# A hybrid decoder block on one core: weight forms kept between the token halves, down thirds alternating, and first-half products on x before its norm

## The chip, the cores and the metric

The kernel runs on one core of one Trainium2 chip. The metric is device time in microseconds (us) of one execution. TensorE is PE in the profile, VectorE is DVE, ScalarE is ACT, GpSimd is POOL, SyncE is SP; SP issues nearly all DMAs.

## The reference

One block over 2048 tokens of width 1024, all in fp32. What matters here:

```
u    = rms_norm(x, norm1_gain)
proj = u @ w_in                      # 1024 -> 3072: lru, gate, q, k, v, g
y_lru = rms_norm(rg_lru(conv4(x_lru)) * gelu(g_lru))
q, k = rotary(q), rotary(k)
y_ret = head_norm(retention(q, k, v)) * silu(g_ret)
h    = x + [y_lru, y_ret] @ w_out
u    = rms_norm(h, norm2_gain)
up   = conv3(u @ ffn_up_w)           # 1024 -> 6144
h    = h + (gelu(a) * v) @ ffn_down_w   # 3072 -> 1024
out  = rms_norm(h, final_norm_gain)
```

The norm of x is a number per token times a gain per channel. A projection is linear, so the number per token may be applied to x or to the projection's output.

## The kernel before

Activations are kept channel-major: a tile has 128 channels on the partitions and 1024 tokens, one half of the sequence (g = 0 or 1). A fp32 product is made of three matmuls on parts: a value is split into a rounded high part (a copy on ACT into the type float32r) and a low part (a subtraction on DVE), and high x high, high x low and low x high are summed in PSUM.

The matrix products are cut into units. A unit multiplies a pair of weight tiles (two groups of 128 output channels, 1024 input channels) with the 1024 tokens of a half. A plain unit (PlainUnit, line 712) does it in eight products of 12 matmuls of 512 columns. A sum-form unit (Unit, line 589) does it in seven, on sums and differences of blocks in the manner of Strassen: its activations are the blocks 11, 21, 22 and the differences T1 to T4 (Blocks, Blocks.put); its weights are one tile as it is (a), two tiles of half sums (s1, s2) and a half tile (v), each split into high and low part (weights, sums). Three low parts and three casts of 1024 columns and four half sums of 512 columns make the forms of one unit, besides v. A unit leaves PSUM through u2, c11, c22, c21 and c12 of PlainOut: ACT copies, and two DVE sums.

The stages follow one another: A (g = 0, four plain units on x times gain, whose outputs are multiplied by the norm's number per token, rb1, while they leave PSUM), AS (g = 0, eight sum-form units, on blocks of the normed x), AS (g = 1, twelve sum-form units), B (output projection, four plain units for each half), U (up projection, 24 sum-form units for each half), D (down projection in three thirds c of the hidden width, four units for each; the three thirds of g = 0, then the three of g = 1). The last unit is plain, in smaller pieces. ORDER names the units of A and AS: l is a channel group of the recurrent branch, q a head's q and k, v a head's v and gate. Every third's partial sum is stored in DRAM and loaded again as the residual of the next (AddOut, partial).

The sum-form blocks of x come from make_x (line 1050): for each pair of tiles it loads x, waits for rb1, multiplies by gain and rb1 on DVE, forms T1 to T4, and stores the seven blocks in DRAM; a stage's bring loads a block, casts and subtracts it.

Nothing of the order is written by hand. A planner (Flow) runs while the program is built: each step is a process with a priority, a tick of 12 matmuls that it is due at, and the planner gives each engine's next instruction by a table of costs and by priority, to 55 slots of 4 KB per partition in SBUF and 8 PSUM banks. The engines then run their instructions in that order, each waiting on semaphores for what it needs. An instruction that PE reaches before its input is there stops PE, since PE takes its matmuls in order.

The lines that matter for the clock of the work:

```
PRODUCTS = ((-4, "p1", "11"), (-2, "p5", "T1"), (0, "p6", "T2"), (1, "p2", "21"), (2, "p7", "T3"),
            (4, "p4", "T4"), (6, "p3", "22"))
```

At the end of a recurrent group (LruGroup.add, line 1163) the sum of squares over four channel groups goes through 16 matmuls of one column (rstd, tile mst), issued on PE among the products.

Of the kernel before, what the change touches and what calls it, by code (L numbers as in the profile page):

```python
# [15 lines left out]

# [1 line left out]

# [14 lines left out]
KT = D // P  # L33
# [19 lines left out]
CH = 4  # L53
ISSUE = 0.45
CL = 100
NDUE = 3
LESS = 0
XSTEP = 6
# [269 lines left out]
def hymba_block_kernel(ctx: ExitStack, tc: tile.TileContext, xh, xn, win, wout, wup, down, gates, vecs,  # L328
# [59 lines left out]
    class Blocks:  # L388
# [2 lines left out]

        names = ("11", "T1", "T2", "21", "T3", "T4", "22")

        def __init__(self, name, more=()):
            self.names = self.names + more
# [155 lines left out]
    class RawStage(Stage):  # L551
# [6 lines left out]
        def bring(self, name, i, need, start):  # L558
# [27 lines left out]
                free(r)  # L586
            self.event(name, i).on = True

    class Unit:


# [4 lines left out]
        def __init__(self, stage, wsrc, out):  # L596
            self.stage, self.wsrc, self.out = stage, wsrc, out
            self.w = {}
            self.there = {n: Event() for n in ("a", "s1", "s2", "v")}
            self.done = {n: Event() for n in ("seed", "u2", "c11", "c22a", "c22b")}  # L600
            out.unit = self

        def weights(self, t0):
            self.t0 = t0
# [83 lines left out]

        def p2(self):
            yield from self.product(self.x, "a", "12", "21", False)  # L690
            free(*self.w["a"])
            fl.spawn(self.out.c11(), self.t0 + 1.9 - SOON)

        def p7(self):
            yield self.done["u2"]
            yield from self.product(self.y, "s1", "3", "T3", False)
            free(*self.w["s1"])
            fl.spawn(self.out.c22(), self.t0 + 2.5 - SOON)

        def p4(self):  # L700
            yield self.done["c22a"]
            yield from self.product(self.y, "v", "v", "T4", False)
            free(self.w["v"])
            fl.spawn(self.out.c21(), self.t0 + 6 - LESS)

        def p3(self):
            yield self.done["c22b"]
            yield from self.product(self.e, "s2", "4", "22", False)
            free(*self.w["s2"])
            fl.spawn(self.out.c12(), self.t0 + 8 - LESS)  # L710

    class PlainUnit:


        period = 8
        quads = ((0, 0), (0, 1), (1, 0), (1, 1))
# [4 lines left out]
        def __init__(self, stage, wsrc, out):  # L721
            self.stage, self.wsrc, self.out = stage, wsrc, out
            self.w = {}
            self.there = [[Event(), Event()] for m in range(2)]
            self.placed = [Event(), Event()]
            out.unit = self
            out.quads = {}

# [48 lines left out]
        def part(self, q, m, n, k, c0=None, c1=None):  # L777
            if c0 is None:
                c0, c1 = n * Q, (n + 1) * Q
            if k == 0:  # L780
                PlainUnit.count += 1
                self.ps = yield Bank(self.tags[PlainUnit.count % 5], "pq")
            yield self.there[m][k]
            bname = f"{k + 1}{n + 1}"
            wh, wl = self.w[m]
            op = None
            for j in range(4):
                if j % 2 == 0:
                    yield self.stage.event(bname, j // 2)
                bh, bl = self.stage.blk[bname, j // 2]  # L790
                c = slice(j % 2 * Q + c0 - n * Q, j % 2 * Q + c1 - n * Q)
                ws = slice((4 * k + j) * P, (4 * k + j + 1) * P)
                for i, (x, y) in enumerate(((wh, bh), (wh, bl), (wl, bh))):
                    mm = pe.matmul(self.ps[:, 0:c1 - c0], x[:, ws], y[:, c], start=k == 0 and j == 0 and i == 0,
                                   stop=k == 1 and j == 3 and i == 2)
                    op = op + mm if op else mm
                if self.halves:
                    yield op
                    op = None
            if op:  # L800
                yield op
            self.stage.used(bname)
            if k == 1:
                if m not in [x[0] for x in self.quads[q + 1:]]:
                    free(*self.w[m])
                fl.spawn(self.leave(m, n, c0, c1), self.t0 + 2 * q + 4 - SOON)

        def leave(self, m, n, c0, c1):
# [28 lines left out]
    class PlainOut:  # L837


        def quadrant(self, m, n, ps):  # L840
# [17 lines left out]
            if (m, 0) in q and (m, 1) in q:  # L858
# [3 lines left out]
                else:  # L862
                    self.t1 = q[m]
                    yield from self.first()

        def u2(self):
# [22 lines left out]
        def c21(self):  # L889
            u = self.unit  # L890
            yield a.copy(self.t2[:, half(0)], u.y)
            free(u.y)
            yield u.done["c22b"]
            yield from self.second()

        def c12(self):
            u = self.unit
            t = self.t1[:, half(1)]
            yield v.tensor_tensor(out=t, in0=t, in1=u.e, op=ALU.add)
            free(u.e)  # L900
            yield u.done["c11"]
            yield from self.first()

    class AddOut:
# [135 lines left out]

    rb1 = {}
    rb_there = [Event() for g in range(NG)]
    rb_left = [KT + 4 * PLAIN] + [KT] * (NG - 1)

    def rb_used(g):
        rb_left[g] -= 1
# [138 lines left out]
    class Head:  # L1185


        def __init__(self, g, h):
            self.g, self.h = g, h
            self.t = {}  # L1190
            self.rope = None
            self.rope_there = Event()
# [2 lines left out]
        def rotate(self, name, x):  # L1195
            sw = yield Slot("sw")
            yield dma(sw[0:64], x[64:128]) + dma(sw[64:128], x[0:64])
            if self.rope is None:
                self.rope = []
                for i in range(2):  # L1200
                    t = yield Slot("rope")
                    self.rope.append(t)
                    yield dma(t, rope[self.g, i])
                self.rope_there.on = True
            yield self.rope_there
            cs, sn = self.rope
# [139 lines left out]
            free(s)  # L1346

    class QkOut(PlainOut):
        def __init__(self, head):
            self.head, self.g = head, head.g  # L1350

# [122 lines left out]
    class UpOut(PlainOut):  # L1474
# [22 lines left out]
        def first(self):  # L1497
# [7 lines left out]
            if self.j % 2 == 0:  # L1505
                even[0] = ca
            else:
                yield t0 + 14
                yield from g_d[self.g][self.j // 8].put(self.j // 2 % 4, even[0], ca)

    even = [None]


    def stage_a(g):
        plain = RawStage("A", g, x_d[g], V_N1)
        st = Stage("AS", g, x_b[g])
        us = []
        group = LruGroup(g)

        def add(i, j, out):  # L1520
            kind, stage = (PlainUnit, plain) if g == 0 and len(us) < PLAIN else (Unit, st)
            us.append(kind(stage, (win[i], win[j]), out))

        heads = [Head(g, h) for h in range(NH)]
        for what in ORDER[g].split():
# [22 lines left out]

    def stage_u(g):
        st = Stage("U", g, u_d[g])  # L1550
        return st, [Unit(st, (wup[j], wup[NF + j]), UpOut(g, j)) for j in range(NF)]

    def stage_d(g, c):
        st = Stage("D", g, g_d[g][c])
# [12 lines left out]
            free(t)  # L1567

        us = []
        for m in range(KT // 2):  # L1570
            ms = (m, m + KT // 2)
            src = [(h_d[g][c][k // 2], k % 2) for k in ms]
            done = (lambda i, t, ms=ms: ng.add(ms[i], t)) if c == 2 else (lambda i, t, ms=ms: partial(ms[i], t))
            out = AddOut(src, done)
            out.pieces = lambda i, t, c0, c1, ms=ms: ng.piece(ms[i], t, c0, c1)
            kind = LastUnit if final and m == KT // 2 - 1 else Unit
# [11 lines left out]
    with tc.manual_schedule():  # L1588
# [2 lines left out]
        fl.spawn(constants(), 3)  # L1591
        table = {}
        end = 0
        last = None
        for i, (st, us) in enumerate(order):
            if last is PlainUnit and type(us[0]) is Unit:
                end += 4
            if st.kind == "A":
                norm1(0, -200, end + NDUE)
                make_x(0, 0, end + XD0)  # L1600
            elif st.kind == "AS" and st.g:
# [96 lines left out]
```

## Time and profile before

| | us |
|---|---|
| median of 3 runs (2181.4 to 2182.86) | 2182.34 |
| the profiled execution | 2183.93 |
| its span, first to last instruction | 2182.1 |
| PE busy | 2152.2 |
| PE weight loads busy | 1773.1 |
| DVE busy | 1764.3 |
| ACT busy | 1245.9 |

The profile is of one execution. A matmul's busy time includes the filling and emptying of the array, so that consecutive matmuls overlap in it. Every instruction is put down to line 127 or 365, the helpers that record them, so that groups are told apart by the names of their tiles: px, py, pe and pq are PSUM tiles of products; wh and wl (wv) high and low parts of weights; bh and raw, bl those of blocks; s a tile of half sums; o an output.

### The profile page before, as it was taken

How to read it: one execution, taken by the hardware profiler on the slowest of the kernel's cores; microseconds unless marked ns; L12 is line 12 of the kernel's file. 1: busy time of each engine (PE TensorE's matmuls, PEld its weight loads, DVE VectorE, ACT ScalarE, POOL GpSimd, SP SyncE). 2: the span in 40 equal slices, each digit the busy share in tenths (PEclk: the TensorE clock that was granted, in tenths of full speed). 3: DMA queues.
4: the chain of work that ended last, by engine and by line, in shares of the span. 5: the costliest groups of instructions: out<-in, count | busy, mean ns of one | idle time of the engine just before them, and what ended most of it. 6: DMA issues, size and time to landing. Idle time of an engine off the chain costs nothing.

```text
span 2182.1 us, 26589 instructions
## 1 busy us (share of the span) xinstructions
PE 2152.2 (99%) x9848; PEld 1773.1 (81%) x9848; DVE 1764.3 (81%) x2227; ACT 1245.9 (57%) x1792; POOL 39.3 (2%) x32
## 2 busy tenths in 40 slices
PE   9999989999999999999999999999999999999998
PEld 6878878888788888888888888888888788888787
DVE  6999888877765688898888898788878987788875
ACT  6774775654852166666666766666666553343441
POOL 0010000000000000000000000000000000000000
PEclk9999999999999999999999999999999999999999
DMA  8966365142647954453224532322335787689662
GB/s 323 373 228 207 109 222 167 61 137 70 224 164 263 374 191 167 166 177 130 100 91 155 193 121 97 116 90 97 112 118 177 264 314 254 227 295 398 230 255 78
DMA packets 142498, 411.00 MB, mean 188 GB/s; under 512 B 16112, under 2 KB 20640, under 8 KB 142368
## 3 DMA queue, kind: packets, MB, share of 16 engines
q1 hardware_dynamic: 141072, 408.25, 52.8%
q8 instruction: 77, 1.26, 0.2%
q10 hardware_dynamic: 1296, 1.05, 0.1%
q14 instruction: 53, 0.43, 0.1%
HBM read 275.78 MB, written 125.07 MB: 184 GB/s over the span
## 4 chain that ended last, share of the span: by engine, by line
PE 94%; DVE 3%; DMA 2%; ACT 1%; POOL 0%; issue 0%; SPq 0%; DVEq 0%
PE py L127 33%; PE px L127 22%; PE pe L127 22%; PE pq L127 12%; PE po L127 1%; DMA raw<-in_dram 1%; PE pa L127 1%; PE pt L127 1%; PE pk L127 1%; PE sc L127 1%; DVE raw L127 1%; PE mst L127 1%; DMA xt<-in_dram 0%; DVE res L127 0%; DMA h<-h 0%
## 5 line engine op out<-in xcount | busy, mean ns | idle before, releaser
L127 DVE TENSOR_TENSOR wl<-s,wh 128x1024 fp32r<-128x1024 f32 x182 | 222.2, 1221 | 108.8 <-ACT wh L127 106.5
L127 PE MATMUL px<-bh,wh 128*128 128x512 f32 x728 | 287.2, 395 | 0.4 <-DVE res L127 0.4
L127 PE MATMUL py<-bh,wl 128*128 128x512 f32 x728 | 284.0, 390 | 2.8 <-DVE wl L127 2.8
L127 PE MATMUL px<-raw,wh 128*128 128x512 f32 x728 | 285.0, 391 | 0.3 <-DVE raw L127 0.3
L127 PE MATMUL py<-bh,wh 128*128 128x512 f32 x728 | 285.2, 392 | 0.0
L127 PE MATMUL pe<-raw,wh 128*128 128x512 f32 x728 | 283.4, 389 | 1.6 <-DVE raw L127 1.6
L127 PE MATMUL pe<-bh,wh 128*128 128x512 f32 x728 | 284.8, 391 | 0.0
L127 PE MATMUL px<-bh,wl 128*128 128x512 f32 x728 | 284.7, 391 | 0.0
L127 PE MATMUL py<-raw,wh 128*128 128x512 f32 x728 | 283.8, 390 | 0.3 <-DVE raw L127 0.3
L127 PE MATMUL pe<-bh,wl 128*128 128x512 f32 x728 | 283.5, 389 | 0.0
L127 ACT CAST wh<-s 128x1024 fp32r<-128x1024 f32 x182 | 190.9, 1049 | 140.8 <-DVE s L127 127.2
L127 DVE SCALAR_TENSOR_TENSOR c<-o,vec,c 128x1022 f32<-128x1022 f32 x192 | 244.1, 1279 | 9.0 <-ACT c L127 4.6
L127 PE MATMUL py<-bh,wv 128*128 128x512 f32 x728 | 240.4, 391 | 3.4 <-ACT o L127 1.7
L127 ACT COPY o<-py 128x512 f32<-128x512 f32 x204 | 119.6, 587 | 198.1 <-PE py L127 197.7
L127 DVE TENSOR_TENSOR raw<-raw,bh 128x1024 fp32r<-128x1024 f32 x158 | 189.2, 1217 | 7.0 <-ACT bh L127 7.0
L127 ACT CAST bh<-raw 128x1024 fp32r<-128x1024 f32 x158 | 161.5, 1048 | 35.7 <-DMA raw<-g_T 14.4
L127 PE MATMUL pq<-bh,wh 128*128 128x512 f32 (+1 forms) x432 | 168.0, 389 | 0.5 <-ACT bh L127 0.4
L127 PEld LDWEIGHTS px<-bh,wh 128*128 128x128 f32 x728 | 137.8, 189 | 35.3 <-issue 3.8
L127 PE MATMUL pq<-bh,wl 128*128 128x512 f32 (+1 forms) x432 | 165.0, 382 | 0.5 <-DVE wl L127 0.5
L127 PEld LDWEIGHTS py<-bh,wv 128*128 128x128 f32 x728 | 136.7, 188 | 34.1 <-ACT o L127 2.2
L127 PEld LDWEIGHTS py<-bh,wl 128*128 128x128 f32 x728 | 136.8, 188 | 31.8 <-DVE wl L127 3.2
L127 PEld LDWEIGHTS px<-bh,wl 128*128 128x128 f32 x728 | 137.5, 189 | 29.0
(143 smaller groups left out, 3819.1 us busy)
## 6 DMA issues: line engine op xcount, KB each, us to landing
wa<-in_dram SPq DMA_DIRECT2D x91, 512.0 KB, 4.6
wb<-in_dram SPq DMA_DIRECT2D x91, 512.0 KB, 5.2
h<-res SPq DMA_DIRECT2D x56, 512.0 KB, 3.4
g_T<-t SPq DMA_DIRECT2D x96, 256.0 KB, 2.5
raw<-g_T SPq DMA_DIRECT2D x48, 512.0 KB, 7.0
res<-h SPq DMA_DIRECT2D x48, 512.0 KB, 7.7
g<-c SPq DMA_DIRECT2D x76, 256.0 KB, 3.4
raw<-g SPq DMA_DIRECT2D x38, 512.0 KB, 7.9
```

Of the source, the lines that this page charges most:

```text
L127: return Op(self.name, lambda: fn(*args, **kw), us, writes, reads, func=func)
```

## The change

Three things change.

1. *Weight forms kept.* If two units that follow one another have the same weight tiles and the same kind, the second takes over the forms of the first (same), which doesn't free them (keep). For this the orders are turned so that the second half starts with the weights that the first half ended with: ORDER, B in reverse for g = 1, U for g = 1 starting with its last two units, D starting with its last. The thirds of D alternate: c = 0 for g = 0, 1; c = 1 for g = 1, 0; c = 2 for g = 0, 1. The pairing of the up projection's outputs (twin) follows.
2. *First-half sum-form units on x without its norm.* For g = 0, make_x multiplies by the gain alone, on ACT, and stores T1 to T4 only; the blocks 11, 21 and 22 are those of the plain units (MixedStage, kind AM), which stay in SBUF. The outputs of the AM units are multiplied by rb1 on DVE after they have left PSUM (times_rb).
3. *Rotary tables normed.* For the q/k units of AM that multiplication is left out and the two rotary tables are multiplied by rb1 once, stored in DRAM and loaded by those heads (scaled_rope).

In ORDER, l3 also moves to the end of the first half.

```diff
-ORDER = ("l0 q0 v0 l1 q1 v1 l2 q2 v2 l3 q3 v3", "l0 q0 v0 l1 q1 v1 q2 v2 l2 q3 v3 l3")
+ORDER = ("l0 q0 v0 l1 q1 v1 l2 q2 v2 q3 v3 l3", "l3 q0 v0 l0 q1 v1 q2 v2 l1 q3 v3 l2")
...
+ROPE_T = 16
...
-    x_b = [Blocks(f"x{g}") for g in range(NG)]
+    x_b = [Blocks(f"x{g}", names=("T1", "T2", "T3", "T4") if g == 0 else None) for g in range(NG)]
+    rope_d = Dram("rope")
...
+    class MixedStage(Stage):
+        def __init__(self, plain, g, src):
+            super().__init__("AM", g, src)
+            self.plain = plain
+            self.blk = ChainMap(self.blk, plain.blk)
+        def event(self, name, i):
+            return (super() if name[0] == "T" else self.plain).event(name, i)
...
+        def same(self, other):
+            self.w, self.there, self.weights = other.w, other.there, self.begin
+            other.keep = True
...
+        def drop(self, *tiles):
+            if not self.keep:
+                free(*tiles)
...
+        def times_rb(self, t):
+            if self.unit.stage.kind == "AM" and not self.scaled:
+                yield rb_there[self.g]
+                yield v.tensor_tensor(out=t, in0=t, in1=rb1[self.g], op=ALU.mult)
+                rb_used(self.g)
...
             yield u.done["c22b"]
+            yield from self.times_rb(self.t2)
             yield from self.second()
...
             yield u.done["c11"]
+            yield from self.times_rb(self.t1)
             yield from self.first()
...
+    def scaled_rope():
+        yield Until(ROPE_T)
+        yield rb_there[0]
+        for i in range(2):
+            t = yield Slot("rope")
+            yield dma(t, rope[0, i])
+            yield v.tensor_tensor(out=t, in0=t, in1=rb1[0], op=ALU.mult)
+            rb_used(0)
+            yield from rope_d.put(i, t)
+            free(t)
...
-            yield rb_there[g]
-            for j in range(2):
-                yield v.scalar_tensor_tensor(out=t[j], in0=t[j], scalar=col(V_N1 + 2 * q + j), in1=rb1[g], op0=ALU.mult, op1=ALU.mult)
-                rb_used(g)
+            if g == 0:
+                for j in range(2):
+                    yield a.activation(t[j], t[j], AF.Copy, scale=gain1[:, 2 * q + j:2 * q + j + 1])
+            else:
...
-                    yield dma(t, rope[self.g, i])
+                    if self.scaled:
+                        yield from rope_d.get(t, i)
+                    else:
+                        yield dma(t, rope[self.g, i])
...
-        st = Stage("AS", g, x_b[g])
+        st = Stage("AS", g, x_b[g]) if g else MixedStage(plain, g, x_b[g])
...
-        for m in range(KT // 2):
+        for m in (range(KT // 2) if g == 0 else reversed(range(KT // 2))):
...
-        return st, [Unit(st, (wup[j], wup[NF + j]), UpOut(g, j)) for j in range(NF)]
+        js = list(range(NF)) if g == 0 else [NF - 1, NF - 2, *range(NF - 2)]
+        return st, [Unit(st, (wup[j], wup[NF + j]), UpOut(g, j)) for j in js]
...
-        for m in range(KT // 2):
+        for m in (range(KT // 2) if g == c % 2 else (KT // 2 - 1, *range(KT // 2 - 1))):
...
-    order += [stage_d(g, c) for g in range(NG) for c in range(3)]
+    order += [stage_d(g, c) for c in range(3) for g in (range(NG) if c != 1 else reversed(range(NG)))]
...
+                if before and type(before) is last and [w.offset for w in before.wsrc] == [w.offset for w in u.wsrc] and \
+                        before.wsrc[0].tensor.name == u.wsrc[0].tensor.name:
+                    u.same(before)
+                before = u
```

## Rows read from the trace of the kernel before

**Rows 1.** The page: busy share of each engine; one group of matmuls.

```profile
PE 2152.2 (99%) x9848; PEld 1773.1 (81%) x9848; DVE 1764.3 (81%) x2227; ACT 1245.9 (57%) x1792; POOL 39.3 (2%) x32
...
L127 PE MATMUL px<-raw,wh 128*128 128x512 f32 x728 | 285.0, 391 | 0.3 <-DVE raw L127 0.3
```

**Rows 2.** Windows: length, busy us (instructions) by engine, PEclk, DMA share, GB/s.

```profile
240.00:280.00 40.00, 40.00 (x218) 34.45 (x217) 38.41 (x67) 23.12 (x30) 2.39 (x2) 1.00 0.40 133
...
880.00:1280.00 400.00, 400.00 (x1767) 331.20 (x1766) 346.52 (x386) 266.07 (x433) 0.00 (x0) 1.00 0.42 144
...
2120.00:2140.00 20.00, 19.24 (x85) 15.59 (x84) 9.44 (x11) 4.58 (x5) 0.00 (x0) 1.00 0.16 53
```

**Rows 3.** Chain of work that ended last: start us, us, what.

```profile
125.01 4.54 PE px L127 x12
147.65 3.48 PE py L127 x10
...
316.69 3.54 PE mst L127 x16
320.24 4.26 PE px L127 x12
...
1707.42 2.73 PE px L127 x12
```

**Rows 4.** PE's waits over the span: us in total, times, longest us.

```profile
PE mst L127 <- DVE sqacc L127: 7.5, 2, 6.3
PE py L127 <- DVE wl L127: 2.8, 1, 2.8
...
PE py L127 <- ACT o L127: 1.7, 1, 1.7
PE py L127 <- DVE res L127: 1.7, 2, 0.9
PE pe L127 <- DVE raw L127: 1.6, 1, 1.6
...
PE pa L127 <- DVE xc L127: 0.9, 1, 0.9
```

**Rows 5.** Narrow windows after two of the waits, columns as in rows 2.

```profile
125.00:130.00 5.00, 5.00 (x15) 3.56 (x16) 5.00 (x7) 2.62 (x5) 0.00 (x0) 0.66 0.60 216
...
320.00:325.00 5.00, 5.00 (x18) 3.97 (x18) 4.72 (x7) 0.46 (x1) 2.01 (x1) 0.69 0.00 0
```

**Rows 6.** DVE by form, 0 to 330 us: count, busy, mean ns, idle before.

```profile
L127 DVE TENSOR_TENSOR raw<-raw,bh 128x1024 fp32r<-128x1024 f32 x26 | 31.1, 1215 | 1.8 <-ACT bh L127 1.7
L127 DVE TENSOR_TENSOR wl<-s,wh 128x1024 fp32r<-128x1024 f32 x19 | 23.1, 1215 | 1.0 <-ACT wh L127 1.0
L127 DVE SCALAR_TENSOR_TENSOR x<-x,vec,rb 128x1024 f32<-128x1024 f32 x16 | 19.9, 1277 | 0.0
...
L127 DVE TENSOR_TENSOR s<-s,wa 128x512 f32<-128x512 f32 x10 | 6.9, 686 | 0.1
```

**Rows 7.** ACT by form, 0 to 330 us, columns as in rows 6.

```profile
L127 ACT CAST bh<-raw 128x1024 fp32r<-128x1024 f32 x28 | 28.5, 1047 | 1.8 <-PE po L127 1.8
...
L127 ACT ACTIVATE ea<-tt,m8sp 128x1024 f32<-128x1024 f32 x4 | 4.6, 1155 | 0.1
```

**Rows 8.** Wide windows, columns as in rows 2.

```profile
40.00:150.00 110.00, 106.16 (x489) 84.06 (x488) 103.15 (x143) 77.36 (x99) 6.26 (x3) 0.98 0.79 287
160.00:320.00 160.00, 153.66 (x761) 126.87 (x759) 137.54 (x204) 103.47 (x137) 4.78 (x4) 0.98 0.58 191
1940.00:2020.00 80.00, 79.31 (x358) 65.14 (x356) 63.77 (x77) 27.60 (x33) 1.64 (x1) 1.00 0.93 353
```

**Rows 9.** DMA issues, 0 to 330 us: count, KB each, median us to landing.

```profile
raw<-x SPq DMA_DIRECT2D x12, 512.0 KB, 7.5
```

**Rows 10.** The page's DMA issues over the span, columns as in rows 9.

```profile
h<-res SPq DMA_DIRECT2D x56, 512.0 KB, 3.4
...
res<-h SPq DMA_DIRECT2D x48, 512.0 KB, 7.7
```

More of the change, by code (lines that the diff above doesn't have):

```diff
@@ L19 @@
+from collections import ChainMap
 from contextlib import ExitStack
@@ L392, in hymba_block_kernel, with __init__ @@
         names = ("11", "T1", "T2", "21", "T3", "T4", "22")
-        def __init__(self, name, more=()):
-            self.names = self.names + more
+        def __init__(self, name, more=(), names=None):
+            self.names = (names or self.names) + more
             self.t = {(n, i): dp.tile([P, 2, Q], F32, name=f"{name}_{n}_{i}", tag=f"{name}_{n}_{i}")
@@ L587, in bring, with uses, used @@
             self.event(name, i).on = True
+    class MixedStage(Stage):
[5 more added lines that the diff above has]
+            return (super() if name[0] == "T" else self.plain).event(name, i)
+        def uses(self, name, tick):
+            (super() if name[0] == "T" else self.plain).uses(name, tick)
+        def used(self, name):
+            (super() if name[0] == "T" else self.plain).used(name)
     class Unit:
@@ L600, in __init__, with begin @@
             self.done = {n: Event() for n in ("seed", "u2", "c11", "c22a", "c22b")}
+            self.keep = False
             out.unit = self
+        def same(self, other):
+            self.w, self.there, self.weights = other.w, other.there, self.begin
+            other.keep = True
+        def begin(self, t0):
+            self.t0 = t0
+        def drop(self, *tiles):
+            if not self.keep:
+                free(*tiles)
         def weights(self, t0):
@@ L690, in p2 @@
             yield from self.product(self.x, "a", "12", "21", False)
-            free(*self.w["a"])
+            self.drop(*self.w["a"])
             fl.spawn(self.out.c11(), self.t0 + 1.9 - SOON)
@@ L696, in p7 @@
             yield from self.product(self.y, "s1", "3", "T3", False)
-            free(*self.w["s1"])
+            self.drop(*self.w["s1"])
             fl.spawn(self.out.c22(), self.t0 + 2.5 - SOON)
@@ L702, in p4 @@
             yield from self.product(self.y, "v", "v", "T4", False)
-            free(self.w["v"])
+            self.drop(self.w["v"])
             fl.spawn(self.out.c21(), self.t0 + 6 - LESS)
@@ L708, in p3 @@
             yield from self.product(self.e, "s2", "4", "22", False)
-            free(*self.w["s2"])
+            self.drop(*self.w["s2"])
             fl.spawn(self.out.c12(), self.t0 + 8 - LESS)
     class PlainUnit:
+        same, begin, drop = Unit.same, Unit.begin, Unit.drop
         period = 8
@@ L725, in __init__ @@
             self.placed = [Event(), Event()]
+            self.keep = False
             out.unit = self
@@ L804, in part @@
                 if m not in [x[0] for x in self.quads[q + 1:]]:
-                    free(*self.w[m])
+                    self.drop(*self.w[m])
                 fl.spawn(self.leave(m, n, c0, c1), self.t0 + 2 * q + 4 - SOON)
@@ L864, in quadrant @@
                     yield from self.first()
+        scaled = False
+        def times_rb(self, t):
[3 more added lines that the diff above has]
+                rb_used(self.g)
         def u2(self):
@@ L1042, in hymba_block_kernel @@
     rb_there = [Event() for g in range(NG)]
-    rb_left = [KT + 4 * PLAIN] + [KT] * (NG - 1)
+    rb_left = [4 * PLAIN + 2] + [KT] * (NG - 1)
+    def scaled_rope():
[8 more added lines that the diff above has]
+            free(t)
     def rb_used(g):
@@ L1059, in one @@
                 t.append(x)
-            yield rb_there[g]
-            for j in range(2):
-                yield v.scalar_tensor_tensor(out=t[j], in0=t[j], scalar=col(V_N1 + 2 * q + j), in1=rb1[g], op0=ALU.mult, op1=ALU.mult)
-                rb_used(g)
+            if g == 0:
+                for j in range(2):
+                    yield a.activation(t[j], t[j], AF.Copy, scale=gain1[:, 2 * q + j:2 * q + j + 1])
+            else:
+                yield rb_there[g]
+                for j in range(2):
+                    yield v.scalar_tensor_tensor(out=t[j], in0=t[j], scalar=col(V_N1 + 2 * q + j), in1=rb1[g], op0=ALU.mult, op1=ALU.mult)
+                    rb_used(g)
             yield from x_b[g].put(q, *t)
@@ L1189, in __init__ @@
             self.g, self.h = g, h
+            self.scaled = False
             self.t = {}
@@ L1348, in hymba_block_kernel @@
     class QkOut(PlainOut):
+        scaled = True
         def __init__(self, head):
@@ L1504, in first @@
             free(self.cv)
-            if self.j % 2 == 0:
-                even[0] = ca
+            if not twin:
+                twin.append(ca)
             else:
                 yield t0 + 14
-                yield from g_d[self.g][self.j // 8].put(self.j // 2 % 4, even[0], ca)
-    even = [None]
+                even, odd = (twin.pop(), ca) if self.j % 2 else (ca, twin.pop())
+                yield from g_d[self.g][self.j // 8].put(self.j // 2 % 4, even, odd)
+    twin = []
     def stage_a(g):
         plain = RawStage("A", g, x_d[g], V_N1)
-        st = Stage("AS", g, x_b[g])
+        st = Stage("AS", g, x_b[g]) if g else MixedStage(plain, g, x_b[g])
         us = []
@@ L1522, in add @@
             us.append(kind(stage, (win[i], win[j]), out))
+            if stage.kind == "AM":
+                if isinstance(out, QkOut):
+                    out.head.scaled = True
+                else:
+                    rb_left[0] += 2
         heads = [Head(g, h) for h in range(NH)]
@@ L1575, in stage_d @@
             out.pieces = lambda i, t, c0, c1, ms=ms: ng.piece(ms[i], t, c0, c1)
-            kind = LastUnit if final and m == KT // 2 - 1 else Unit
+            kind = LastUnit if final and m == KT // 2 - 2 else Unit
             us.append(kind(st, (down[c, ms[0]], down[c, ms[1]]), out))
@@ L1593, in hymba_block_kernel @@
         end = 0
-        last = None
+        last = before = None
         for i, (st, us) in enumerate(order):
@@ L1600, in hymba_block_kernel @@
                 make_x(0, 0, end + XD0)
+                fl.spawn(scaled_rope(), ROPE_T + 6)
             elif st.kind == "AS" and st.g:
```

## The prediction

> **What bounds the kernel now.** The page's share table comes first: TensorE (PE) is busy for 99% of the span, VectorE (DVE) for 81% [rows 1]. In the long middle stretch, the up projection, PE issues 1767 matmuls in 400 us with no idle time [rows 2], and in the chain of waits twelve 512-column matmuls, one product, take 2.73 us [rows 3]. A sum-form unit (seven products) is thus 7 x 2.73 = 19.1 us and a plain one (eight) 21.8 us, whatever the other engines do. The change neither adds nor removes a product. All it can give is what PE loses around its products.
>
> A matmul is shown busy for 0.39 us [rows 1] while a product advances by one per 2.73/12 = 0.23 us, so the 99% hides losses, and the next views look for them. PE's list of waits names the larger ones [rows 4]; the chain and the narrow windows place them and add what the slower clock costs after some:
>
> A, near 123 us: 0.9 us for a convolution output [rows 4], then a product takes 4.54 instead of 2.73 us [rows 3], at a granted clock of 0.66 [rows 5], part of it at the lower of the two levels. Loss 0.9 + 1.8 = 2.7 us.
> B, just before 148 us: 2.8 us for a weight's low part from DVE [rows 4], then 10 matmuls in 3.48 instead of 2.28 us [rows 3]. Loss 2.8 + 1.2 = 4.0 us.
> C, before 317 us: 6.3 us for the sum of squares of the first half's recurrent group [rows 4], before its 16 small matmuls, then 4.26 instead of 2.73 us for a product [rows 3] at a clock of 0.69 [rows 5]. Loss 6.3 + 1.5 = 7.8 us.
> D, at the end of the second half's projection: 1.7 us for an ACT copy [rows 4].
> E, start of the down projection: 1.6 us for a block's low part, 0.9 us for a residual sum [rows 4]; 2.5 us.
> F, 1940 to 2020 us, where the first half's final norm runs beside the second half's first down third: PE busy 79.3 of 80 us [rows 8]; 0.7 us.
> G, last unit: the other 0.8 us of the residual waits [rows 4].
> Together 20.2 us. The start and the tail after the last product are not touched by the edits.
>
> The Trainium skill ("Perfetto Trace Analysis", section Identifying the Most-Contended Engine) says that matmul busy share is a poor measure of the distance from the bound and weight-load busy share a better one. By the rule, as an estimate, the 1773.1 us of weight loads at the middle stretch's 0.83 would fill 2141 us and leave 41 us; by the busy share 30 us are left; this trace bears the rule out as far as the 99% hid the losses above.
>
> **The change, part by part.**
>
> *First-half sum-form units on x without its norm.* Off DVE: 8 scalings of x at 1277 ns (half of the row's 16), 10.2 us, and 6 low parts of the blocks 11, 21 and 22 at 1215 ns, 7.3 us [rows 6]. Onto DVE: two rotary tables early, and one multiply of 1024 columns for both outputs of the five AM units that are not q/k units (v1, l2, v2, v3, l3), spread over some 110 to 350 us. At 1215 ns, the row of a two-tensor operation of that size [rows 6], that is 2.4 and 10 x 1.215 = 12.2 us. On ACT 6 casts of 1047 ns go, 6.3 us; 8 scalings by a column come, at 1155 ns like the activations scaled by a column [rows 7], 9.2 us; the net 2.9 us is hidden while ACT is busy for 77 of 110 us [rows 8], and without that cover would delay a block by as much. So by 150 us DVE is relieved of 10.2 + 7.3 - 2.4 = 15.1 us, where it was busy for 103 of 110 us [rows 8]. B is a wait of 2.8 us for a DVE instruction with 15.1 us taken out ahead of it: I take it as gone (bounds: gone, or as it is if later work is planned into the room). A waits for a longer chain over ACT and DVE: I take half, 1.3 us (bounds 0 and 2.7).
>
> A rule speaks against moving the scaling: the Trainium skill ("ScalarE: Activation LUTs", section Rules for kernel authors) gives multiplication to VectorE, as the faster engine. By it ACT would pay more than DVE is spared, A and B could stay, and the sum below would be 4.3 instead of 9.6 us; here the scaling is not faster on DVE, 1277 ns against 1155 ns [rows 6, 7], so the row decides against the rule.
>
> *Its DMAs, on SP's queue.* Gone are 12 stores of 256 KB and 6 loads of 512 KB, 6.3 MB; two rotary tables in and out add 2.1 MB. At the 287 GB/s of 40 to 150 us [rows 8] the net 4.2 MB are 15 us of transfer. No wait of PE there is for a DMA, so I count zero. The q heads' rotary loads come from the kernel's own store, written long before; were that late, a load's landing of 7.5 us [rows 9] would show.
>
> *Weight forms kept.* At six boundaries (projection, output, up, three down thirds) the second half's first unit uses the forms of the unit before. A sum-form unit spares DVE three low parts at 1215 ns, four half sums and the v part at about 686 ns: 3.6 + 3.4 = 7.1 us [rows 6]; ACT three casts and a half, 3.7 us [rows 7]; SP two loads, 1 MB. The output projection's plain unit spares two low parts, 2.4 us. This gives time only where PE waits for DVE near a boundary: after C and at F. In the up projection PE never idles: zero.
>
> *The order within the projection.* With l3 last, the first half's group norm and C's 16 small matmuls come about two units (38 us) later, among the second half's units. C is an in-order PE stopped by a DVE chain that ran 6.3 us behind its planned time. Bounds: gone (7.8 back), or the full price again plus the two new multiplies ahead of it (2.4 us worse). I take half, 3.9 us back, because DVE has 7.1 us less to do at just that boundary. D keeps its shape (an l unit ends the stage): zero, bounds 1.7 either way.
>
> *Thirds alternating over the halves.* A partial result is reloaded at least three units (57 us) after it is stored instead of four; store and load take 3.4 + 7.7 us [rows 10], so nothing shows; without the cover the load's 7.7 us would. The first half's final norm and output (8 loads and 8 stores of 512 KB, 8 scalings) move from under the second half's first third to under its last, the final 80 us, where DVE was busy for 9.4 of 20 us and the DMA engines for 0.16 [rows 2]. F moves with them; with 7.1 us of DVE spared there I take half back, 0.4 us (bounds: all 0.7, or 0.7 worse). E and G as they are.
>
> **Sum.** 4.0 + 1.3 + 3.9 + 0.4 = 9.6 us. The profiled execution took 2183.9 us (span 2182.1, 1.8 around it), 1.6 above the median of 2182.3; 2183.9 - 9.6 = 2174.3 for its like, 2172.7 for the median. I say 2173.
>
> **The rivals.**
>
> *All the listed losses go.* 2182.3 - 20.2 = 2162. For it: relief of 7 to 15 us of DVE ahead of A, B, C and F. Against it: D, E and G wait behind work that the change leaves alone. Chance 0.13.
>
> *No change.* PE's order is fixed by a planner with its own costs; where DVE runs late against them, a wait comes back one place on: the room that B leaves is filled with blocks of the second half, and C recurs two units later. 2182, within 4. For it: C was 6.3 us late although DVE had idle time in that stretch (137.5 of 160 us busy [rows 8]). If kept forms are not reused as described, the same comes out. Chance 0.19.
>
> *Slower, by DVE between 160 and 320 us.* There 137.5 of 160 us are busy [rows 8], and 38.4 of the 40 from 240 on [rows 2]; 12.2 us of multiplies come in. While the second half's scalings and differences can be put off, DVE keeps ahead. The point that decides: when more than the 1.6 us free in the tightest 40 falls due inside them, a weight form is late and PE stops as at C, slow clock included. One such stop more, B gone: 2182.3 - 4.0 + 7.8 = 2186; two, 2194. Against it: the multiplies come after the copies that free PSUM, so no product waits for them itself, and DVE enters the stretch 15 us lighter. Chance 0.15.
>
> **How the numbers follow.** The forecast has 0.53. A measurement of this kernel can tell 0.2%, 4.4 us, from no change. Below 2178 lie the forecast, the large gain and a little of the no-change case, 0.68; up to 2186.7 lies 0.18; above it 0.14. The likeliest case alone spans 2165 to 2178. The whole range begins at 2160 (all listed losses, and half of the 3.54 us of C's small matmuls [rows 3], should they too have run at the lower clock level: 2162 - 1.8) and ends at 2187, one new stop of C's size and F doubled; outside lie two such stops, or gains with no source that I see.
>
> **What would show it.** Right: the matmul count unchanged; the wait for the low part near 148 us gone and no clock below 0.9 there; the wait for the sum of squares near 350 us and shorter than 6.3 us; no PE wait above 1 us in the last 80 us. Wrong: a new wait of several us for a weight or a block between 160 and 400 us; a last unit held up by the first half's stores; B still there, which would say that DVE's load was not its cause.

## The result, and the profile after

The changed kernel takes 2169.7 us (median of 4 runs, 2168.0 to 2171.6) against 2182.6: a ratio of 0.9936, with a 95% interval of 0.9924 to 0.9949, 12.9 us less. Forecast were 2173 and a range of 2160 to 2187. The two profiled executions took 2183.9 and 2169.8 us; their spans, 2182.1 and 2168.0 us, differ by 14.1 us.

The page of the changed kernel, the lines that answer to [rows 1]:

```profile
span 2168.0 us, 26431 instructions
...
PE 2146.2 (99%) x9848; PEld 1770.4 (82%) x9848; DVE 1728.9 (80%) x2183; ACT 1227.4 (57%) x1769; POOL 41.0 (2%) x32
```

PE has the same 9848 matmuls. DVE has 44 instructions and 35 us less to do, over the whole span. PE's busy share reads 99% in both profiles, so it does not show the gain; the weight loads' share rises from 81 to 82%. The Trainium skill ("Perfetto Trace Analysis", section Identifying the Most-Contended Engine) says that matmul busy share is not a good measure of the distance from the bound, and these two shares agree. What has changed is in PE's waits, those that [rows 4] listed (us in total, times, longest):

```profile
PE pe L129 <- DVE o L129: 2.0, 2, 1.2
PE py L129 <- DVE res L129: 1.9, 1, 1.9
PE py L129 <- ACT o L129: 1.7, 1, 1.7
...
PE pe L129 <- DVE raw L129: 1.6, 1, 1.6
...
PE pt L129 <- DVE o L129: 1.2, 1, 1.2
PE mst L129 <- DVE sqacc L129: 1.2, 1, 1.2
```

The low part of 2.8 us (B), the convolution output of 0.9 us (A) and the 6.3 us for the sum of squares (C) are gone; the 1.2 us that is left for a sum of squares is in the tail, as it was. D (ACT, 1.7 us) and the 1.6 us of E stand as they were. New are waits for an output on DVE. The same three windows in both kernels say where the time went (columns as in [rows 2]); the kernel before:

```profile
40.00:200.00 160.00, 156.16 (x728) 125.95 (x727) 148.25 (x203) 101.18 (x130) 6.26 (x3) 0.98 0.75 270
200.00:300.00 100.00, 100.00 (x500) 81.50 (x499) 83.30 (x139) 66.10 (x93) 4.78 (x4) 1.00 0.55 174
300.00:470.00 170.00, 163.66 (x798) 135.01 (x797) 136.84 (x198) 107.57 (x143) 6.41 (x5) 0.97 0.41 132
```

and the changed kernel:

```profile
40.00:200.00 160.00, 159.49 (x772) 130.95 (x773) 141.75 (x198) 102.78 (x132) 4.87 (x3) 1.00 0.73 252
200.00:300.00 100.00, 96.85 (x473) 79.00 (x472) 85.69 (x136) 60.04 (x85) 5.59 (x4) 0.98 0.54 182
300.00:470.00 170.00, 170.00 (x847) 138.83 (x846) 141.22 (x209) 112.95 (x150) 7.81 (x5) 1.00 0.35 114
```

Before 200 us PE is idle for 0.5 instead of 3.8 us and its clock is full; from 300 to 470 us it is not idle at all, where 6.3 us were. From 200 to 300 us it is now idle for 3.2 us, where it was never idle, and its clock is 0.98. That place, in the chain of the changed kernel, in a narrow window, and on DVE:

```profile
251.72 4.60 PE pe L129 x12
```

```profile
250.00:255.00 5.00, 4.23 (x16) 3.32 (x16) 4.96 (x7) 4.35 (x7) 0.00 (x0) 0.70 0.00 0
```

```profile
248.51 1.23 DVE L129 TENSOR_TENSOR o<-o,sw 128x1024 f32<-128x1024 f32 x1
...
250.98 0.68 DVE L129 TENSOR_TENSOR o<-o,pe 128x512 f32<-128x512 f32 x1
```

PE waits 1.2 us for the rotary result of 248.51 us before eight transpositions, and 0.8 us behind them for the sum of 250.98 us, which empties the PSUM tile pe that the next product fills. That product then takes 4.60 instead of 2.73 us, much as A's did (4.54): the granted clock over these 5 us is 0.70, part of it at the lower of the two levels. The third new wait, 1.2 us near 205 us, is for such a sum too.

### The profile page after: what moved, and what is told of

Read it like the earlier page. It is cut to its first block, busy times and chain, and to the rows that moved or that the text cites. A ratio compares the mean times of both kernels' runs of the same rounds, so it can differ in the third digit from the quotient of the medians.

```text
span 2168.0 us, 26431 instructions
## 1 busy us (share of the span) xinstructions
PE 2146.2 (99%) x9848; PEld 1770.4 (82%) x9848; DVE 1728.9 (80%) x2183; ACT 1227.4 (57%) x1769; POOL 41.0 (2%) x32
## 4 chain that ended last, share of the span: by engine, by line
PE 95%; DVE 2%; DMA 2%; ACT 0%; POOL 0%; issue 0%; SPq 0%; DVEq 0%
PE py L129 34%; PE px L129 22%; PE pe L129 22%; PE pq L129 12%; PE po L129 1%; DMA raw<-in_dram 1%; PE pa L129 1%; PE pt L129 1%; PE sc L129 1%; PE pk L129 1%; PE mst L129 0%; DMA xt<-in_dram 0%; DMA w<-in_dram 0%; DVE res L129 0%; DVE o L129 0%; POOL ms L129 0%
## 5 line engine op out<-in xcount | busy, mean ns | idle before, releaser
L129 DVE TENSOR_TENSOR wl<-s,wh 128x1024 fp32r<-128x1024 f32 x172 | 210.3, 1223 | 118.8 <-ACT wh L129 110.7
L129 PE MATMUL pe<-raw,wh 128*128 128x512 f32 x696 | 271.2, 390 | 1.6 <-DVE raw L129 1.6
L129 PE MATMUL px<-raw,wh 128*128 128x512 f32 x664 | 258.7, 390 | 0.0
L129 ACT CAST wh<-s 128x1024 fp32r<-128x1024 f32 x172 | 180.4, 1049 | 108.4 <-DVE s L129 102.6
L129 ACT CAST bh<-raw 128x1024 fp32r<-128x1024 f32 x152 | 156.1, 1050 | 65.9 <-DMA raw<-g_T 34.8
L129 DVE TENSOR_TENSOR raw<-raw,bh 128x1024 fp32r<-128x1024 f32 x152 | 182.3, 1219 | 9.8 <-ACT bh L129 9.7
L129 PEld LDWEIGHTS pe<-bh,wh 128*128 128x128 f32 x728 | 137.2, 188 | 32.3 <-DVE o L129 2.9
L129 PEld LDWEIGHTS py<-bh,wh 128*128 128x128 f32 x728 | 136.8, 188 | 31.9 <-ACT o L129 1.5
```

The costliest lines, as they stand in the source:

```text
L129: return Op(self.name, lambda: fn(*args, **kw), us, writes, reads, func=func)
```

## The experiments

Each kernel ran beside the kernel before on its chip; the medians of before were 2183.2, 2183.3 and 2182.7 us in the three groups. The first four take the change apart: orders alone, orders with kept forms, the raw x alone, orders with raw x.

**Orders alone.**

```diff
-                    u.same(before)
+                    pass
...
-        st = Stage("AS", g, x_b[g]) if g else MixedStage(plain, g, x_b[g])
+        st = Stage("AS", g, x_b[g])
```

(and make_x, the block names and rb's count for g = 0 as before, no scaled_rope)

> Only the turned orders (projection, output, up, down with alternating thirds); no weight forms are kept, x is normed before its blocks as before. DVE's work is that of before. Theory (DVE load): A and B stay, since nothing is taken off DVE ahead of them (wait for the low part near 148 us within 1 us of 2.8); only C can move with the l3 unit: 2174 to 2183. Rival (order): C was a matter of where the group norm stands, so most of the gain is here already: about 2173, wait for the sum of squares under 1 us. Rival (replanning): any new plan scatters the waits; A and B change too although DVE has the same to do.

Measured: 2180.7 us, ratio 0.9989 (0.9980 to 0.9998). PE's waits, with the low part near 148 us among them:

```profile
PE py L129 <- ACT o L129: 5.9, 3, 2.4
...
PE py L129 <- DVE wl L129: 2.7, 1, 2.7
```

B stays at 2.7 us, A at 0.5; C is gone, and two ACT copies make PE wait instead, 2.4 us near 353 us and 1.7 us near 449 us. The number is the theory's, inside its range, and not the rival's: moving the group norm does not bring the gain.

**Orders and kept forms.** As above, with `u.same(before)` in force:

```diff
-        st = Stage("AS", g, x_b[g]) if g else MixedStage(plain, g, x_b[g])
+        st = Stage("AS", g, x_b[g])
```

> Turned orders and kept weight forms, x normed before its blocks as before. Theory: A and B stay; C is gone, with 7.1 us of DVE spared behind the first half: about 2175. Against the run with the orders alone the forms give 0 to 4 us. Rival (order): no difference from the run with the orders alone, within 2 us. Rival (replanning): A and B differ from before.

Measured: 2181.5 us, ratio 0.9986 (0.9977 to 0.9995), no better than the orders alone. B is there with 2.7 us, and the largest wait is 4.1 us for an ACT copy near 376 us:

```profile
PE py L129 <- ACT o L129: 7.1, 3, 4.1
...
PE py L129 <- DVE wl L129: 2.7, 1, 2.7
```

My 2175 was wrong: C was gone by its name, and a wait of 4.1 us stood three units (59 us) further on.

**Raw x alone.** The orders of before in ORDER, B, U and D, the rest as in the change; no two neighbouring units share weights.

```diff
-ORDER = ("l0 q0 v0 l1 q1 v1 l2 q2 v2 q3 v3 l3", "l3 q0 v0 l0 q1 v1 q2 v2 l1 q3 v3 l2")
+ORDER = ("l0 q0 v0 l1 q1 v1 l2 q2 v2 l3 q3 v3", "l0 q0 v0 l1 q1 v1 q2 v2 l2 q3 v3 l3")
...
```

> Only the first half's sum-form units on x without its norm, outputs and rotary tables normed; the orders are those of before, so no forms can be kept. Theory: A and B gone (6.7 us), C still there with its 6 to 8 us: about 2176. Rival (order): A and B alone, C untouched, the same number, but then the orders alone must give the rest. Rival (slower by DVE between 160 and 320 us): new PE waits for weights there, over 2182.

Measured: 2183.1 us, ratio 0.9998 (0.9989 to 1.0007). Its windows and its largest wait:

```profile
40.00:200.00 160.00, 159.86 (x775) 131.20 (x775) 141.56 (x199) 102.42 (x131) 4.87 (x3) 1.00 0.73 253
200.00:300.00 100.00, 96.85 (x472) 77.55 (x471) 85.84 (x140) 69.35 (x94) 4.78 (x4) 1.00 0.52 174
300.00:470.00 170.00, 161.43 (x784) 132.70 (x783) 140.32 (x202) 102.77 (x140) 8.42 (x5) 0.96 0.38 124
```

```profile
PE mst L129 <- DVE sqacc L129: 8.0, 2, 6.8
```

A and B are gone, as the theory had it (PE idle for 0.1 us before 200 us). But C is 6.8 us, the new waits from 200 to 300 us are there, and an ACT copy near 449 us adds 1.7 us, so that nothing is left of the gain.

**Orders and raw x, no forms kept.**

```diff
-                    u.same(before)
+                    pass
```

> The whole change but with no weight forms kept: each unit makes its own. Theory: A and B gone, C moved two units later and partly there, F as before: 2171 to 2176, slower than the whole change by 1 to 5 us. Rival (order): same as the whole change, 2170, within 2 us: keeping the forms brings nothing by itself.

Measured: 2183.9 us, ratio 1.0004 (0.9995 to 1.0013), which neither expectation had. A and B are gone; PE waits 1.9 us for a block near 333 us, 4.8 us for a weight's low part near 385 us, 1.7 us for an ACT copy near 451 us. DVE ahead of the 4.8 us (start, us, instruction, the idle time before it and what ended it):

```profile
371.73 1.23 DVE L129 TENSOR_TENSOR o<-o,rope 128x1024 f32<-128x1024 f32 x1 [3.48 <-DMA rope<-in_dram]
...
381.25 2.35 DVE L129 TENSOR_TENSOR_SCAN xc<-ea,hlast,gi 128x1024 f32<-128x1024 f32 x1
383.64 0.15 DVE L129 COPY hlast<-xc 128x1 f32<-128x1 f32 x1
383.72 1.23 DVE L129 TENSOR_TENSOR wl<-s,wh 128x1024 fp32r<-128x1024 f32 x1
```

DVE takes its instructions in the order given. It stands for 3.5 us before a rotary multiply whose table hasn't landed, goes through a run that ends with the scan of 2.35 us, and only then makes the low part that PE needs.

So the parts do not add up. By the ratios the four kernels gain 2.4, 3.1, 0.4 and -0.9 us, and the whole change 14 us. The next four runs ask whether the forms matter at one boundary or at six, and whether the full gain is an accident of one plan.

**Forms kept at the projection's boundary alone.**

```diff
-                    u.same(before)
+                    if st.kind in ("AS", "AM"):
+                        u.same(before)
```

> The whole change with weight forms kept at the projection's boundary alone (the l3 unit), made anew at the other five. Theory (the forms of that one unit take away the stop of 4.8 us and its slow clock near 380 us that the run without kept forms has): 2170 to 2174, no PE wait over 1.5 us between 320 and 400 us. Rival (the forms at the later boundaries matter): 2180 or more. Rival (replanning): the front as in the whole change, since the plan up to there is the same.

Measured: 2170.6 us, ratio 0.9944 (0.9932 to 0.9957), all of the gain within the interval, and no idle time of PE from 300 to 470 us:

```profile
300.00:470.00 170.00, 170.00 (x849) 139.24 (x848) 141.19 (x209) 113.04 (x150) 7.81 (x5) 1.00 0.36 115
```

One unit's forms, l3's, turn 2183.9 into 2170.6 us; the other five boundaries bring nothing that can be measured. Up to 290 us this kernel has the waits of the changed one at the same places (within 0.8 us), so it is no second plan of the front.

**The changed kernel with its due time shifted,** and **the kernel before with the same shift**: the same instructions, planned anew.

```diff
-XD0 = 10
+XD0 = 12
```

> The changed kernel with the due time of the first half's x blocks two ticks later (XD0 12 for 10): the same instructions in a somewhat other order. Theory (less load): A, B and C stay away, within 3 us of the changed kernel, 2167 to 2173. Rival (a fortunate plan): a stop of 4 to 9 us comes back somewhere between 300 and 460 us, 2174 to 2183.

> The kernel before with the same shift of the due time (XD0 12 for 10), the same instructions. Theory: A, B and C within 2 us of before, 2180 to 2186. Rival (a fortunate plan): the time moves by over 4 us either way, and C or B is gone.

Measured: 2171.8 us, ratio 0.9943 (0.9929 to 0.9956), for the changed kernel and 2184.8 us, ratio 1.0006 (0.9997 to 1.0015), for the one before. The changed kernel keeps its gain, though its waits have moved (the new ones between 200 and 300 us are now one of 3.4 us for a low part near 236 us). In the kernel before they have moved too, B to 4.4 us near 237 us and C to 4.6 us for a block near 315 us:

```profile
PE py L127 <- DVE raw L127: 5.7, 3, 4.6
PE py L127 <- DVE wl L127: 4.4, 1, 4.4
```

The theory is right about the times and wrong about the places: a wait belongs to a plan. In this one test the time stays with the kernel, within 2.1 us. With the shift, A and B are gone from their places without the raw x too: from 40 to 200 us PE is idle for 2.0 us, in smaller waits.

**The changed kernel with the thirds in the order of before.**

```diff
-        for m in (range(KT // 2) if g == c % 2 else (KT // 2 - 1, *range(KT // 2 - 1))):
+        for m in range(KT // 2):
...
-    order += [stage_d(g, c) for c in range(3) for g in (range(NG) if c != 1 else reversed(range(NG)))]
+    order += [stage_d(g, c) for g in range(NG) for c in range(3)]
```

> The changed kernel with the down projection in the order of before (three thirds of the first half, then of the second, no forms kept there). Theory: F is back (about 0.7 us and up to 2), the wait in the last unit is 0.8 instead of 1.9 us: within 2 us of the changed kernel, 2168 to 2172. Rival (alternating thirds carry part of the gain): 2174 or more. The front half of the trace is that of the changed kernel.

Measured: 2171.3 us, ratio 0.9944 (0.9932 to 0.9957): the same. F is back with 0.6, 0.3 and 0.4 us, and the last unit waits 0.8 instead of 1.9 us. Alternating the thirds is worth nothing that can be measured.

The last four ask what it is in the l3 unit's forms, and price the change's own additions.

**The l3 unit's loads put back.** In `begin`, for stage AS:

```diff
+            def loads():
+                yield Until(t0 - LEAD)
+                ra = yield Slot("wa")
+                yield dma(ra, self.wsrc[0])
+                rb = yield Slot("wb")
+                yield dma(rb, self.wsrc[1])
+                yield t0 - 6 - WB
+                free(ra, rb)
```

> The changed kernel, but the second half's first projection unit (l3) loads its two raw weight tiles as it did, 1 MB on SP's queue, and uses neither: it still takes over the kept forms. Theory (what the kept forms spare is DVE and ACT time): as the changed kernel, 2168 to 2173. Rival (it is the DMA queue: in the run without kept forms DVE waited 3.5 us for a rotary load ahead of the stop near 380 us): the stop comes back, 2178 to 2184.

**Its DVE and ACT work put back,** without the loads:

```diff
+            def work():
...
+                yield a.copy(hi, self.w["a"][0].bitcast(F32))
+                yield low(lo, x, hi)
...
+                yield a.copy(h2, s1)
+                yield low(l2, s1, h2)
...
```

> The changed kernel, but beside the kept forms that l3 unit has the DVE and ACT work of making forms done again on scratch tiles at the times it had (three low parts, four half sums, a half low part: 7.1 us of DVE; three casts and a half on ACT), with no loads; nothing uses the result. Theory (DVE and ACT time): the stop near 380 us comes back, with its slow clock 5 to 9 us, 2176 to 2184. Rival (the DMA queue): as the changed kernel, 2168 to 2173.

Measured: 2176.6 us, ratio 0.9972 (0.9962 to 0.9982), with the loads; 2182.8 us, ratio 1.0001 (0.9992 to 1.0010), with the work. The work takes the whole gain back, as the theory had it, and the loads half of it, which neither the theory nor its rival had: the forms spare two things, and each put back alone brings a stop. Each edit also holds slots of SBUF again (two for the loads, five for the work), so that the work on DVE, that on ACT, the loads and the slots are not told apart in full. With the work, PE's larger waits are those of the kernel without kept forms, one for one: 1.9 us near 334, 4.5 near 387 and 1.7 near 452 us. In both, DVE waits for a rotary load first and PE for the low part behind the scan, 3.5 us near 380 us and 4.5 us near 387 us. The stop with the loads leaves the clock at 1.00 from 380 to 390 us, and after that with the work it is 0.52 from 387 to 392 us. DVE with the loads:

```profile
368.77 1.23 DVE L129 TENSOR_TENSOR o<-o,rope 128x1024 f32<-128x1024 f32 x1 [3.68 <-DMA rope<-in_dram]
...
376.03 2.35 DVE L129 TENSOR_TENSOR_SCAN xc<-ea,hlast,gi 128x1024 f32<-128x1024 f32 x1
378.42 0.15 DVE L129 COPY hlast<-xc 128x1 f32<-128x1 f32 x1
378.50 1.23 DVE L129 TENSOR_TENSOR wl<-s,wh 128x1024 fp32r<-128x1024 f32 x1
```

and in the changed kernel, where the low part that was late there has been made long before the scan and DVE's wait for a table is 1.7 us:

```profile
369.11 1.22 DVE L129 TENSOR_TENSOR wl<-s,wh 128x1024 fp32r<-128x1024 f32 x1
...
379.39 1.23 DVE L129 TENSOR_TENSOR sw<-sw,rope 128x1024 f32<-128x1024 f32 x1 [1.69 <-DMA rope<-in_dram]
...
384.31 2.35 DVE L129 TENSOR_TENSOR_SCAN xc<-ea,hlast,gi 128x1024 f32<-128x1024 f32 x1
```

**No multiply of the outputs by the norm.**

```diff
-                yield v.tensor_tensor(out=t, in0=t, in1=rb1[self.g], op=ALU.mult)
```

The AM units' v, gate and recurrent outputs lack the norm's number per token.

> The changed kernel without the ten multiplies of the AM units' outputs by the norm's number per token, which are left out of the computation for those units. Theory (these 12.2 us of DVE are the price of the change): the two new stops, near 204 and 250 us, go: 2164 to 2168. Rival (off every product's path, they cost nothing): 2169 to 2172.

Measured: 2174.4 us, ratio 0.9960 (0.9947 to 0.9972), which neither expectation had: slower than the changed kernel by 4.7 us, with 11.3 us less of DVE work. The new waits between 200 and 300 us are gone, as expected; but PE waits 1.8 us for an ACT copy near 365 us and 2.9 us near 372 us for a low part, behind the same rotary multiply (1.8 us late) and scan.

**The scaling of x on DVE.**

```diff
-                    yield a.activation(t[j], t[j], AF.Copy, scale=gain1[:, 2 * q + j:2 * q + j + 1])
+                    yield v.tensor_scalar(out=t[j], in0=t[j], scalar1=gain1[:, 2 * q + j:2 * q + j + 1], scalar2=None, op0=ALU.mult)
```

> The changed kernel with the eight scalings of x by the gain on DVE, as one-source operations with a scalar per partition, in place of ACT. By the prediction's reasoning (1155 ns on ACT against 1277 on DVE) DVE loses 8 to 10 us of its relief and waits of 3 to 5 us come back before 200 us: 2173 to 2178. Rival (the one-source form is faster than the two-source one: 486 ns for 512 columns in the trace before, so some 0.8 us for 1024): 6 us more of DVE work, little of it felt, 2169 to 2173.

Measured: 2179.2 us, ratio 0.9984 (0.9975 to 0.9993). The one-source operation takes 746 ns (instruction, count, minimum/median/maximum ns, first and last start):

```profile
L129 DVE TENSOR_SCALAR x<-x,gain x8: 744/746/748, 36.0 to 83.2; 128x1024 f32<-128x1024 f32 x8
```

The rival's duration was right and its time wrong; the first expectation had the wait, and its range ended 1.2 us too early. 6.0 us more of DVE work before 90 us bring B back (3.8 us near 144 us) and a wait of 4.6 us near 242 us:

```profile
PE py L129 <- DVE wl L129: 8.4, 2, 4.6
```

## Why the prediction was right, and where not

The direction, the size and the bound were right: PE's products are untouched, and what went is waits and slow clock around them in the projection. The sum behind the size was not: it added the parts as if each kept its worth alone. By its terms the raw x alone should have given 5.3 us (A and B); it gave 0.4. Point by point, with the losses that the prediction listed:

*A and B*, forecast 1.3 of 2.7 and 4.0 of 4.0 us: both gone. The cause named, DVE's load up to 150 us, is shown from three sides for this due time: without the raw x, B is there with 2.7 us in both kernels (orders, with and without forms); with raw x and the scaling on ACT, PE is idle for at most 1 us from 40 to 200 us in every kernel here; and with 6.0 us of load put back, a wait of 3.8 us is there again. With the due time shifted and no raw x, B is no longer near 148 us, and one of 4.4 us stands near 237 us, so that the place is the plan's matter.

*C*, forecast half of 7.8 us: all of it is gone, with the slow clock after it. This step was mis-sized (3.9 us), and its reason held only in part. The kept l3 forms do decide over this place (2183.9 against 2170.6 us), but only together with the raw x: with the forms and no raw x a wait of 4.1 us is there as well.

*New waits*: 1.2 us near 205 us, 1.2 and 0.8 us and a slow product (4.60 - 2.73 = 1.9 us) near 250 us; 5.1 us that the sum put at zero. The slower rival had the place (between 160 and 320 us) right and the size wrong. That the multiplies cause them is likely and not shown: they go without the ten multiplies, but also with the shifted due time and with the scaling on DVE, where the multiplies stay. Late is no weight form, as the rival had it, but mostly the sum that empties a PSUM tile; the reason against this rival, that the multiplies come after what frees PSUM, did not keep that sum early. The same waits stand in all seven kernels here that have the multiplies, the scaling on ACT and the unshifted due time; the slow product behind them does not (see the last section).

*F* went altogether (0.7 us, forecast 0.4), G rose from 0.8 to 1.9 us (forecast unchanged): on DVE the low parts of the last unit's weights stand right before a residual sum, and the first half's scalings ahead of them. Both are the alternation's, and with the old order they change back, so that it nets nothing. One of the prediction's signs fails with G: a wait of 1.9 us stands in the last 80 us, where none above 1 us was to be. Of E 0.9 us went; D stood.

Added up: 2.7 + 4.0 + 7.8 + 0.7 + 0.9 gone, 5.1 + 1.1 come, 9.9 us. These are numbers of the two profiled executions, whose spans differ by 14.1 us, so 4.2 us are not in the list. Of them 2.4 us are slow clock that the prediction's list left out. In the kernel before, the second product after B takes 3.46 instead of 2.73 us:

```profile
151.13 3.46 PE px L127 x12
```

And C's 16 small matmuls take 3.54 us there [rows 3], in the changed kernel

```profile
365.42 1.84 PE L129 MATMUL mst<-ones,sqacc 128*128 128x1 f32 x16
```

The other 1.8 us are not placed. So the forecast of 9.6 us came close partly by luck: A, C, E and F gave 6.5 us more than the sum had for them, and the new waits and G took 6.2 us that it had at zero.

*The reasoning on ACT and DVE* chose the wrong row. 1277 ns was a two-source operation with gain and norm in one; the gain alone takes 746 ns on DVE and 1145 on ACT:

```profile
L129 ACT ACTIVATE x<-x,gain 128x1024 f32<-128x1024 f32 x8 | 8.9, 1145 | 0.3 <-DMA x<-in_dram 0.2
```

The Trainium skill ("ScalarE: Activation LUTs", section Rules for kernel authors) gives multiplication to VectorE as the faster engine per element, with a figure for bf16; by the durations this trace, in fp32, agrees with it, against what the prediction said. By the kernel's time it does not carry over: with the scaling on DVE the kernel is some 10 us slower (ratios to before of 0.9984 against 0.9936), and the waits that come back there are for DVE.

*No change*, the rival by replanning, was right about four of the kernels and wrong about this one. A wait does come back further on, near 353, 376 and 385 us, in the three partial kernels with turned orders; in the fourth C stays where it was, near 310 us. That it did not in the changed one holds for two more plans: the shifted one and, from 300 us on, the one that scales on DVE. (The variants without alternating thirds and without the later forms have the front of the changed kernel's plan and do not count as plans of their own.) But it is no matter of DVE's load alone: the kernel without the multiplies has less load, a stop near 372 us and 4.7 us more. How often other plans of the changed kernel would keep the gain was not tried beyond one shift.

What is shown of that stop: PE waits for a low part that DVE makes behind a rotary multiply and a scan; the multiply waits 1.8 to 3.7 us for its table, in four kernels (no forms, loads, work, no multiplies). The planner's own formula lets a 512 KB load land 1.7 us and 512/330 us after its issue, 3.3 us, if no other load is ahead of it; in these kernels the tables took 5 to 8 us, in the changed one 3.5 to 5.8:

```profile
DMA to landing us min/median/max: 7.9/7.9/7.9
```

(with the loads put back, the tables from 300 to 460 us). What landing time the planner reckoned for these loads is not on record. That it reckons too short, that this is the cause, and a truer landing time the cure, is argued and not shown: no kernel with another landing time was run. Why the plan of the changed kernel puts the low part ahead of the scan and the others do not stays open as well.

## What to carry to other kernels

Price a change to a planned, in-order kernel as a whole: here the parts gave 0 to 3 us each and 13 together, so measuring parts one by one would have thrown them all away. Work on the engine that the bound waits for can cost more than its own microseconds, because a stop may also cost clock: here 6.0 us put back on DVE cost some 10 us, and one unit's form work, 7.1 us of DVE and 3.7 us of ACT, cost 13. It need not: taking 11.3 us off DVE elsewhere made this kernel 4.7 us slower. A slower instruction on an engine with room beat a faster one on that engine. Plan the same instructions again with a shifted constant, more than once if differences of 5 us matter, before a gain is put down to the kernel and not to one order.

## What was not expected of the hardware

The clock fell after short waits, and not each time. In the changed kernel two waits of 1.2 and 0.8 us, with eight small transpositions between them, came with a granted clock of 0.70 over 5 us; A's 0.9 us had been followed by 0.66 [rows 5]. After the 1.7 us at D the clock stays at 1.00 (558 to 563 us). Neither the length of the wait nor the small matmuls around it settle this: with the raw x alone the same two waits stand at the same place among the same matmuls, and the clock stays full:

```profile
250.00:255.00 5.00, 4.23 (x25) 3.45 (x24) 4.96 (x6) 4.11 (x7) 0.00 (x0) 1.00 0.00 0
```

Of the seven kernels with these two waits, four show 0.66 to 0.70 in this window and three (raw x alone, orders and raw x, loads put back) show 1.00. The same holds for B: after its 2.7 us the clock is 0.66 from 149 to 154 us with the orders alone, and with the kept forms added

```profile
149.00:154.00 5.00, 5.00 (x24) 4.10 (x23) 4.96 (x8) 0.93 (x2) 0.00 (x0) 1.00 0.94 349
```

So the price of a short wait is not fixed: near 250 us the product behind it takes 1.9 us more or it does not. Each trace shows one execution; what decides, and whether it changes from one execution of a kernel to the next, stays open.
